# Short-band attention: one transpose for both key blocks, and projections in a planned line of quarters

## The chip, the cores and the metric

The kernel runs on one core of one Trainium2 chip. The metric is the device time of one execution in microseconds; the kernel before took 903.53 us (median of three runs, 901.57 to 904.65).

## What is computed

One block of a transformer over 1024 tokens of width 1024, in float32: a modulated RMS norm, one input projection, two kinds of attention, their gated outputs, and an output projection. Attention A (8 heads in 2 groups) has three branches: compressed, selected, and a window of 512. Attention B, the short band, is the part that the change touches (8 heads in 2 groups of 4, window 128, one learned sink a head):

```
dist  = qpos - kpos
valid = (dist >= 0) & (dist < 128) & (kpos >= 0)
s = q k^T / 8 - slope * dist            where valid, else -1e30
p = softmax([s, sink])[..., :-1]
o = p v
```

A block of 128 queries meets two blocks of 128 keys, the one ahead of it and its own. Query p of the block sees the keys j > p of the block ahead and the keys j <= p of its own: of every two keys at the same column j exactly one is in the window.

## The kernel before

**Numbers.** The products are float32 made of two parts: each operand is split into a high part (rounded to float32r, "hh", "wh", "kh", "ph") and the rest ("hl", "wl", "kl", "pl"). A projection of one half (512 tokens) of one weight block is 24 matmuls of 512 columns: eight slices of the input width times three products (L187, L194, L195). A weight block comes by DMA in two halves of 256 KB (wraw), ACT makes the high part (L161) and POOL the rest (L164). There are three buffers for wraw and six each for wh and wl.

**Units.** Attention runs in four units: B group 0, B group 1, A group 0, A group 1. A unit goes through query blocks i = 0 to 7; a step is one block and branch. `scores` does, for each of the four heads: two matmuls q times kh and kl (L770, L773; 256 columns for B), a DVE reduction that adds the distance table, writes the negated row to SBUF and takes its minimum (L780), and an exponential with row sum on ACT (L792). For B the sink is then brought in by two DVE sums of four columns and an exponential of four columns (L798 to L801), and POOL scales the four rows by the reciprocal (L804). `weigh` then takes each key block: four transposes by TensorE into one bank (L841), the high part by ACT (L847), the rest by DVE (L848), and two matmuls of 512 columns with V into the bank pv (L849, L852). A B step with i > 0 has two key blocks, so eight transposes and four such matmuls. `finish` adds the two halves of pv (L861, L862), multiplies by a gate on POOL (L863) and stores. Of PSUM's banks three are for scores, two for transposes, one for pv and two for projections. Row tiles: tag ps, 4 buffers of 1024 columns, and pw, 4 of 640; the B steps took ps and pw in turn.

**Order.** The order on each engine is fixed before the run by a scheduler with priorities. Scores of step i go ahead of the transposes and products of step i-1, at high priority. Into this go projections that later steps and units need, and gate projections (merge) that are only stored. A planner keeps a clock of attention work (`done`, columns / 2400) and notes in `mark` the matmul at each point. `held(t)` gives the matmul behind which a projection has to stay; `owed` makes a later matmul of the attention stay behind a projection. In the A units a line of projections is cut into quarters (six matmuls each) that are spread over the unit: quarter() keeps each of them behind the attention matmul 3 us of that clock ahead of its place and in front of the one 4 later:

```
            hold[0] = held(at - AHEAD)
...
            owed.append((at + LAG, ins))
```

In the B units whole projections of a half were put behind certain steps instead (`at_step`, `k_fills`, `q_fills`), eight in either unit, three of them merges, with the first bound and without the second.

Of the kernel before, what the change touches and what calls it, by code (L numbers as in the profile page):

```python
# [7 lines left out]
F32 = mybir.dt.float32  # L8
F32R = mybir.dt.float32r
# [5 lines left out]
P = 128  # L15
# [6 lines left out]
LATE = (0.1, 0.1)  # L22
LAG = 4
# [3 lines left out]
AHEAD = 3  # L27
# [41 lines left out]
def hybrid_kernel(tc, io, out):  # L69
# [601 lines left out]
    def load_tables(mixer):  # L671

        tab = at.tile([P, HS + P], F32, name="tab", tag="tab", bufs=1)
        if mixer == "B":
            nc.scalar.dma_start(tab[:, :256], io["DB"])
            tables["DB"] = tab[:, :256]
        else:
            nc.scalar.dma_start(tab[:, : HS + 120], io["DA"])
            tables["DW"], tables["DCMP"] = tab[:, :HS], tab[:, HS : HS + 120]
# [31 lines left out]
    def scores(mixer, g, i, br):  # L711
# [9 lines left out]
        else:  # L721
# [22 lines left out]
            "slc": ("ps", S), "win": ("pw", 640), "cmp": ("pc", 0), "swa": (("ps", S), ("pw", 640))[i % 2]}[br]  # L744
        for r in range(4):
            h = 4 * g + r
            pump()
            if len(rows) < 4:
                q = Q[(mixer, h, half)][:, qo : qo + P]
                row = at.tile([P, width], F32, name=tag, tag=tag, bufs=4)  # L750
                off = 0
                for c, (kh_half, b0, nb) in enumerate(parts):
# [12 lines left out]
                    elif br == "win":  # L765
                        dist = tables["DW"][:, :w]
                    else:
                        d0 = (b0 - (i - 1)) * P
                        dist = tables["DB"][:, d0 : d0 + w]
# [8 lines left out]
                    else:  # L778
                        init = BIGF
                    ins = nc.vector.tensor_tensor_reduce(  # L780
# [4 lines left out]
                    if pre:  # L785
# [41 lines left out]

    def weigh(mixer, g, i, br, tiles, pv, first, last):

        rows, b0 = tiles  # L830
        if br == "cmp":
            weigh_pairs(g, rows, pv)
            return
# [43 lines left out]
    class Planned:  # L877
# [13 lines left out]
        def quarter(self, k, at, nxt):  # L891
# [5 lines left out]
            hold[0] = held(at - AHEAD)  # L897
# [8 lines left out]
            owed.append((at + LAG, ins))  # L906
# [11 lines left out]
    def plan_k(g, half):  # L918
# [6 lines left out]
    n_late = len(late)  # L925
    late_done = [0]
# [6 lines left out]
    for mixer, g in units:  # L933
        columns = 0
        for i in range(NT):
            for br in ["swa"] if mixer == "B" else ["slc", "win", "cmp"]:
                nb = {"swa": min(i, 1), "slc": i, "win": min(i, 4), "cmp": 0}[br] + 1
                columns += 1650 if br == "cmp" else 2048 * nb + 8 * (nb * P + 64 * (br == "slc"))
        whole.append(columns / 2400)

    for u, (mixer, g) in enumerate(units):
# [5 lines left out]
        nt = len(tasks)  # L947
        at_step = {}

        def spread(fs, lo, hi):  # L950
            for n, f in enumerate(fs):
                at_step.setdefault(int(lo + (hi - lo) * n / len(fs)), []).append(f)

        if mixer == "B":
            own = [] if u == 1 else k_fills(mixer, g, 1)
            spread(own + q_fills(mixer, g, 1), 0, 3 * nt // 8)
            m2, g2 = units[u + 1]
            nk = k_fills(m2, g2, 0) if m2 == "A" else []
            spread(nk + q_fills(m2, g2, 0), nt // 2, nt)
        else:  # L960
# [7 lines left out]
            for n, f in enumerate(line):  # L968
                nxt = next((x for x in line[n + 1 :] if x.w is not f.w), None)
                for k in range(4):  # L970
                    pieces.append((begun + whole[u] * (n + k / 4) / len(line),
                                   lambda at, f=f, k=k, nxt=nxt: f.quarter(k, at, nxt)))
# [11 lines left out]
        for n, (i, br) in enumerate(tasks):  # L984
# [22 lines left out]
        with tc.high_priority(offset=PRIO):  # L1007
            second(prev)
        for at, f in pieces:
            f(at)  # L1010
# [245 lines left out]
```

## Time and profile before

| | |
|---|---|
| median of three runs | 903.53 us |
| profiled execution: its own time | 904.5 us |
| its span | 902.7 us |
| PE busy | 893.1 us (99%) |
| DVE, ACT, POOL busy | 539.0, 504.0, 354.8 us |
| mean granted TensorE clock | 0.999 |

The span goes from the first to the last instruction in the trace; the rest of the execution's own time lies around it. Matmuls are pipelined: a row gives 0.39 us for one matmul of 512 columns where the next starts 0.23 us later, so the cost of one is read from the distance of starts. PEld is the loading of weights into TensorE, beside the matmuls.

### The profile page before, as it was taken

Reading aid. Unit: us, or ns where it says so; the run is one execution under the profiler, and the core shown is the slowest. Engines: PE = TensorE matmul, PEld = TensorE weight load, DVE = VectorE, ACT = ScalarE, POOL = GpSimd, SP = SyncE. Lnnn points to the kernel's source line nnn. Section 1 sums busy time; section 2 is a strip of 40 time slices with the busy share of each in tenths; the row PEclk is TensorE's granted clock in tenths of the full one; section 3 lists DMA queues with packets and bytes.
Section 4 is the critical chain, followed back from the end, with each engine's and each line's share of the span. In section 5 each row is a group of like instructions: output and inputs, shape, how many; then the busy total and the mean of one; then the engine's idle time right before and its main releaser. Section 6 shows DMA issues by size and latency. Waiting matters only on the chain.

```text
span 902.7 us, 14354 instructions
## 1 busy us (share of the span) xinstructions
PE 893.1 (99%) x4568; PEld 755.4 (84%) x4568; DVE 539.0 (60%) x1514; ACT 504.0 (56%) x1151; POOL 354.8 (39%) x422
## 2 busy tenths in 40 slices
PE   9999999999999999999999999999999999999997
PEld 7888888888888888888888888888887888887885
DVE  5866763455678577675575577566464362677322
ACT  5467632466587677665666687565564565431111
POOL 0000522364576776443445566443442376100000
PEclk9999999999999999999999999999999999999999
DMA  8873342242234322112212131211202577334432
GB/s 317 297 266 100 129 164 97 86 147 95 82 105 132 102 80 68 51 47 71 71 59 71 68 93 58 70 49 47 82 36 71 208 254 233 112 126 167 134 108 78
DMA packets 66942, 104.51 MB, mean 116 GB/s; under 512 B 7985, under 2 KB 25777, under 8 KB 66866
## 3 DMA queue, kind: packets, MB, share of 16 engines
q1 hardware_dynamic: 65712, 102.36, 34.0%
q10 hardware_dynamic: 1154, 1.23, 0.5%
q8 instruction: 36, 0.59, 0.3%
q14 instruction: 40, 0.33, 0.1%
HBM read 79.97 MB, written 19.92 MB: 111 GB/s over the span
## 4 chain that ended last, share of the span: by engine, by line
PE 99%; DVE 0%; ACT 0%; issue 0%; DVEq 0%; POOLq 0%; ACTq 0%
PE b_pt L841 8%; PE b_pj L900 7%; PE b_pj L904 7%; PE b_pj L905 7%; PE b_pj L187 6%; PE b_pj L195 6%; PE b_pj L194 6%; PE b_s L773 5%; PE b_s L770 4%; PE b_pv L852 4%; PE b_pv L849 4%; PE b_s L1139 1%; PE b_s L1141 1%; PE b_s L1140 1%; PE b_pt L294 1%; PE b_s L1063 1%
## 5 line engine op out<-in xcount | busy, mean ns | idle before, releaser
L164 POOL TENSOR_TENSOR wl<-wraw,wh 128x512 fp32r<-128x512 f32 x102 | 135.2, 1326 | 141.0 <-ACT wh L161 87.9
L848 DVE TENSOR_TENSOR pl<-b_pt,ph 128x512 fp32r<-128x512 f32 x162 | 110.3, 687 | 65.3 <-ACT ph L847 64.5
L847 ACT CAST ph<-b_pt 128x512 fp32r<-128x512 f32 x162 | 93.6, 583 | 64.0 <-PE b_pt L841 51.1
L900 PE MATMUL b_pj<-hh,wh 128*128 128x512 f32 x288 | 117.6, 412 | 0.0
L905 PE MATMUL b_pj<-hh,wl 128*128 128x512 f32 x288 | 114.0, 396 | 0.0
L904 PE MATMUL b_pj<-hl,wh 128*128 128x512 f32 x288 | 113.1, 394 | 0.0
L187 PE MATMUL b_pj<-hh,wh 128*128 128x512 f32 x240 | 94.6, 394 | 1.7 <-DVE gates L244 1.7
L194 PE MATMUL b_pj<-hl,wh 128*128 128x512 f32 x240 | 94.6, 394 | 0.0
L195 PE MATMUL b_pj<-hh,wl 128*128 128x512 f32 x240 | 94.4, 393 | 0.0
L804 POOL TENSOR_SCALAR ps<-ps,rr,gates 128x128 f32<-128x128 f32 (+7 forms) x64 | 52.4, 823 | 94.6 <-DVE rr L796 54.6
L770 PE MATMUL b_s<-kh,q 128*128 128x256 f32 (+6 forms) x272 | 85.4, 322 | 0.2 <-DVE minc L786 0.2
L773 PE MATMUL b_s<-kl,q 128*128 128x256 f32 (+6 forms) x272 | 83.7, 315 | 0.0
L792 ACT ACTIVATE ps<-ps,mins 128x256 f32<-128x256 f32 (+7 forms) x96 | 64.9, 677 | 30.1 <-DVE mins L780 28.4
L161 ACT CAST wh<-wraw 128x512 fp32r<-128x512 f32 x94 | 57.7, 616 | 38.3 <-PE b_pj L194 14.8
L792 ACT ACTIVATE pw<-pw,mins 128x256 f32<-128x256 f32 (+4 forms) x96 | 60.7, 632 | 28.2 <-DVE mins L780 26.6
L852 PE MATMUL b_pv<-pl,V 128*128 128x512 f32 x162 | 67.8, 418 | 0.3
L849 PE MATMUL b_pv<-ph,V 128*128 128x512 f32 x162 | 65.7, 405 | 0.0
L905 PEld LDWEIGHTS b_pj<-hh,wl 128*128 128x128 f32 x288 | 54.1, 188 | 10.8
L904 PEld LDWEIGHTS b_pj<-hl,wh 128*128 128x128 f32 x288 | 54.4, 189 | 8.5
L804 POOL TENSOR_SCALAR pw<-pw,rr,gates 128x640 f32<-128x640 f32 (+4 forms) x64 | 47.3, 742 | 32.9 <-DVE rr L796 25.4
L900 PEld LDWEIGHTS b_pj<-hh,wh 128*128 128x128 f32 x288 | 53.9, 189 | 7.5
L841 PE MATMUL b_pt<-ident,ps 128*128 128x128 f32 x344 | 57.8, 272 | 0.0
(303 smaller groups left out, 2106.9 us busy)
## 6 DMA issues: line engine op xcount, KB each, us to landing
wraw<-in_w_blk SPq DMA_DIRECT2D x90, 256.0 KB, 2.7
wa<-in_w_adaT SPq DMA_DIRECT2D x24, 512.0 KB, 5.2
w1raw<-in_w SPq DMA_DIRECT2D x16, 256.0 KB, 3.6
od<-ot SPq DMA_DIRECT2D x64, 64.0 KB, 2.1
sp_MA<-sp SPq DMA_DIRECT2D x16, 256.0 KB, 2.0
wraw<-in_w_o SPq DMA_DIRECT2D x16, 256.0 KB, 3.0
wraw<-in_w_out SPq DMA_DIRECT2D x16, 256.0 KB, 3.0
t<-od SPq DMA_DIRECT2D x16, 256.0 KB, 3.9
```

The source lines that it names most:

```text
L164: chain("wl", nc.gpsimd.tensor_tensor(wl, raw, wh.bitcast(F32), ALU.subtract))
L187: ins = nc.tensor.matmul(t, lhsT=wh, rhs=hh[kc][half], start=(kc == 0), stop=False)
L194: nc.tensor.matmul(t, lhsT=wh, rhs=hl[kc][half], start=False, stop=False)
L195: nc.tensor.matmul(t, lhsT=wl, rhs=hh[kc][half], start=False, stop=(kc == KC - 1))
L770: ins = nc.tensor.matmul(sp[:, :n_in], lhsT=q, rhs=rh, start=True, stop=False)
L773: nc.tensor.matmul(sp[:, :n_in], lhsT=q, rhs=rl, start=False, stop=True)
L792: nc.scalar.activation(rows[r][:, :off], rows[r][:, :off], AF.Exp, scale=-1.0, bias=last_min[:, r : r + 1], accum_out=sums[:, r : r + 1])
L841: ins = nc.tensor.transpose(t[:, r * P : r * P + P], rows[r][:, off : off + P], ident)
L848: nc.vector.tensor_tensor(pl, t, ph.bitcast(F32), ALU.subtract)
L900: ins = nc.tensor.matmul(self.t, lhsT=wh, rhs=hh[kc][self.half], start=(kc == 0), stop=False)
L904: nc.tensor.matmul(self.t, lhsT=wh, rhs=hl[kc][self.half], start=False, stop=False)
L905: ins = nc.tensor.matmul(self.t, lhsT=wl, rhs=hh[kc][self.half], start=False, stop=(kc == KC - 1))
```

## The change

For a B step with i > 0 the two score blocks are joined before the reduction: DVE copies, by a mask (j > p), the scores of the block ahead over those of the block itself, in PSUM, so that the reduction, exponential, scaling and transposes deal with 128 columns for each head where they had 256. After the transposes ACT and DVE write the high part and the rest side by side into one tile of 1024 columns, and POOL parts it by two `affine_select` into the keys of the block ahead and those of the own block, with zeros elsewhere. Four matmuls of 512 columns follow, as before. The two new tiles are of tag ps; the four rows of a B step now lie in one buffer of pw.

The projections in the B units go by the line of quarters of the A units, with bounds of their own (1.5 us ahead, 2 behind): seven in the first unit, nine in the second, the merges six in all as before. The place of a quarter within its projection moves by a fifth of a quarter in all units. The planner counts a joined weighing as 3100 columns. The distance table of B becomes one block of 128 columns and the mask beside it.

```diff
-LATE = (0.1, 0.1)
-LAG = 4
 WARM = (7, 14, 8, 4)
 KEEP = 2
 WBUFS = 6
-AHEAD = 3
+
+AHEAD = {"B": 1.5, "A": 3}
+LAG = {"B": 2, "A": 4}
 PRIO = 1500
...
             nc.scalar.dma_start(tab[:, :256], io["DB"])
-            tables["DB"] = tab[:, :256]
+            tables["DB"] = tab[:, :P]
+            tables["first"] = tab[:, P : 2 * P].bitcast(mybir.dt.int32)
...
-            "slc": ("ps", S), "win": ("pw", 640), "cmp": ("pc", 0), "swa": (("ps", S), ("pw", 640))[i % 2]}[br]
+            "slc": ("ps", S), "win": ("pw", 640), "cmp": ("pc", 0), "swa": ("pw", 640)}[br]
+        if br == "swa":
+            four = at.tile([P, width], F32, name=tag, tag=tag, bufs=4)
         for r in range(4):
             h = 4 * g + r
             pump()
             if len(rows) < 4:
                 q = Q[(mixer, h, half)][:, qo : qo + P]
-                row = at.tile([P, width], F32, name=tag, tag=tag, bufs=4)
+                row = four[:, r * P : r * P + P] if br == "swa" else at.tile([P, width], F32, name=tag, tag=tag, bufs=4)
...
-                        d0 = (b0 - (i - 1)) * P
-                        dist = tables["DB"][:, d0 : d0 + w]
+                        dist = tables["DB"]
...
+                    if br == "swa" and i:
+
+                        nc.vector.copy_predicated(sp[:, P : 2 * P], tables["first"], sp[:, :P])
+                        pre, w = P, P
...
+    def weigh_joined(g, i, rows, pv):
+
+        pump()
+        t = bank("pt")
+        for r in range(4):
+            ins = nc.tensor.transpose(t[:, r * P : r * P + P], rows[r][:, :P], ident)
+            if r == 0:
+                chain("pt", ins)
+                mark(ins, 3100)
+        own, ahead = (at.tile([P, S], F32R, name="pj", tag="ps", bufs=4) for _ in range(2))
+        nc.scalar.copy(own[:, :512], t)
+        nc.vector.tensor_tensor(own[:, 512:], t, own[:, :512].bitcast(F32), ALU.subtract)
+
+        nc.gpsimd.affine_select(
+            out=ahead, in_=own.bitcast(F32), pattern=[[0, 8], [-1, P]], compare_op=ALU.is_gt, fill=0.0,
+            base=0, channel_multiplier=1)
+        nc.gpsimd.affine_select(
+            out=own, in_=own.bitcast(F32), pattern=[[0, 8], [1, P]], compare_op=ALU.is_ge, fill=0.0,
+            base=0, channel_multiplier=-1)
+        for n, (part, b) in enumerate(((ahead, i - 1), (own, i))):
+            v = V[b][:, 4 + g].rearrange("p a d -> p (a d)")
+            for k in range(2):
+                ins = nc.tensor.matmul(
+                    pv, lhsT=v, rhs=part[:, 512 * k : 512 * k + 512], start=(n == 0 and k == 0),
+                    stop=(n == 1 and k == 1))
+                if n == 0 and k == 0:
+                    chain("pv", ins)
...
+        if br == "swa" and i:
+            weigh_joined(g, i, rows, pv)
+            return
...
-            hold[0] = held(at - AHEAD)
+            hold[0] = held(at - AHEAD[mixer])
...
-            owed.append((at + LAG, ins))
+            owed.append((at + LAG[mixer], ins))
...
-                columns += 1650 if br == "cmp" else 2048 * nb + 8 * (nb * P + 64 * (br == "slc"))
+                weighed = 1650 if br == "cmp" else 3100 if br == "swa" and i else 2048 * nb
+                columns += weighed + (0 if br == "cmp" else 8 * (nb * P + 64 * (br == "slc")))
...
-        if mixer == "B":
-            own = [] if u == 1 else k_fills(mixer, g, 1)
-            spread(own + q_fills(mixer, g, 1), 0, 3 * nt // 8)
-            m2, g2 = units[u + 1]
-            nk = k_fills(m2, g2, 0) if m2 == "A" else []
-            spread(nk + q_fills(m2, g2, 0), nt // 2, nt)
+        if u == 0:
+            line = plan_k(g, 1, "B") + plan_q("B", 0, 1) + merges(2) + plan_q("B", 1, 0)
+        elif u == 1:
+            line = plan_q("B", 1, 1) + merges(2) + plan_k(0, 0) + merges(2) + plan_q("A", 0, 0)
...
+        places = [n / len(line) for n in range(len(line) + 1)]
+        if u == 0:
+            places = [0.1 * n if n < 4 else 0.3 + 0.7 * (n - 3) / (len(line) - 3) for n in range(len(line) + 1)]
+        for n, f in enumerate(line):
+            nxt = next((x for x in line[n + 1 :] if x.w is not f.w), None)
+            for k in range(4):
+                spot = places[n] + (places[n + 1] - places[n]) * (k + 0.2) / 4
+                pieces.append((begun + whole[u] * spot,
+                               lambda due, f=f, k=k, nxt=nxt, mixer=mixer: f.quarter(k, due, nxt, mixer)))
...
-            hold[0] = held(done[0] - AHEAD)
-            for f in at_step.get(n, []):
-                f()
-            now = done[0] - begun
-            while mixer == "B":
-
-                part = ((late_done[0] + 0.5) / n_late - sum(LATE[:u])) / LATE[u]
-                if part > 1 or part * whole[u] > now:
-                    break
-                hold[0] = held(begun + part * whole[u] - AHEAD)
-                late.pop(0).whole()
-                late_done[0] += 1
...
-    j = np.arange(256)[None, :]
-    d = 128 + p - j
-    DB = dist(d, (d < 0) | (d >= 128))
+
+    j = np.arange(P)[None, :]
+    DB = np.concatenate([np.where(j > p, p - j + P, p - j), j > p], axis=1).astype(np.float32)
```

## Rows read from the trace of the kernel before

**Rows 1.** The page's first two parts: busy us of PE, and the granted clock.
```profile
PE 893.1 (99%) x4568; PEld 755.4 (84%) x4568; DVE 539.0 (60%) x1514; ACT 504.0 (56%) x1151; POOL 354.8 (39%) x422
...
PEclk9999999999999999999999999999999999999999
```

**Rows 2.** All waits of PE in the span: us in total, times, longest us.
```profile
PE b_pj L187 <- DVE gates L244: 1.7, 1, 1.7
PE b_pt L294 <- DVE eps L309: 1.0, 1, 1.0
PE b_s L770 <- DVE minc L786: 0.2, 1, 0.2
```

**Rows 3.** Busy us and instructions of each engine in the short-band units, then PEclk, DMA.
```profile
162.00:298.00 136.00, 136.00 (x717) 115.00 (x716) 83.04 (x252) 89.12 (x243) 81.52 (x107) 1.00 0.34 106
```

**Rows 4.** The chain of waits, 160 to 310 us: start us, us, what.
```profile
232.28 0.87 PE b_pt L841 x8
```

**Rows 5.** Timeline of PE, start and us: projections, then scores.
```profile
205.09 0.39 PE L187 MATMUL b_pj<-hh,wh 128*128 128x512 f32 x1
...
207.81 0.39 PE L187 MATMUL b_pj<-hh,wh 128*128 128x512 f32 x1
...
213.54 0.28 PE L770 MATMUL b_s<-kh,q 128*128 128x256 f32 x1
...
214.13 0.28 PE L773 MATMUL b_s<-kl,q 128*128 128x256 f32 x1
```

**Rows 6.** POOL's groups by shape, whole span: count | busy us, mean ns | idle before.
```profile
L164 POOL TENSOR_TENSOR wl<-wraw,wh 128x512 fp32r<-128x512 f32 x102 | 135.2, 1326 | 141.0 <-ACT wh L161 87.9 <-DVE wh L158 33.7 <-PE b_pt L615 7.3
L863 POOL TENSOR_TENSOR ot<-ot,zt 64x512 f32<-64x512 f32 x32 | 41.2, 1287 | 41.7 <-DVE ot L862 41.4 <-DMA wraw<-in_w_blk 0.2
...
L804 POOL TENSOR_SCALAR pw<-pw,rr 128x256 f32<-128x256 f32 x32 | 14.7, 479 | 15.8 <-DVE rr L801 10.9 <-PE b_pv L852 3.5 <-PE b_s L773 1.4
...
L804 POOL TENSOR_SCALAR ps<-ps,rr,gates 128x1024 f32<-128x1024 f32 x8 | 9.6, 1202 | 21.6 <-DVE rr L796 21.6
...
L804 POOL TENSOR_SCALAR ps<-ps,rr 128x128 f32<-128x128 f32 x8 | 2.8, 371 | 3.5 <-DVE rr L801 2.6 <-ACT wh L161 0.9
masks.py:199 POOL TENSOR_SCALAR_AFFINE_SELECT ident<-ident 128x128 f32<-128x128 f32 x1 | 0.3, 292 | 0.1
...
L1248 POOL MEMSET const-bfloat16-1.0<- 128x1 bf16 x1 | 0.1, 101 | 0.0
```

**Rows 7.** DVE's groups by shape, 100 to 310 us, same columns.
```profile
L780 DVE CUSTOM_DVE_ANT_0 pw<-b_s,tab,nsink 128x256 f32<-128x256 f32 x32 | 14.7, 477 | 8.7 <-PE b_s L773 8.5
...
L798 DVE TENSOR_TENSOR rr<-mins,nsink 128x4 f32<-128x4 f32 x16 | 8.4, 527 | 0.5
...
L780 DVE CUSTOM_DVE_ANT_0 ps<-b_s,DC,nsink 128x128 f32<-128x128 f32 x8 | 2.6, 345 | 3.4 <-PE b_s L773 3.3
...
L652 DVE CAST vc<-vcf 128x128 fp32r<-128x128 f32 x2 | 0.4, 224 | 0.0
```

**Rows 8.** Timelines of POOL and DVE: start us, us, engine, line, what.
```profile
228.21 1.84 POOL L804 TENSOR_SCALAR ps<-ps,rr 128x256 f32<-128x256 f32 x4 [1.48 <-DVE rr L801]
...
273.70 1.29 POOL L863 TENSOR_TENSOR ot<-ot,zt 64x512 f32<-64x512 f32 x1 [0.98 <-DVE ot L862]
274.06 2.21 DVE L798 TENSOR_TENSOR rr<-mins,nsink 128x4 f32<-128x4 f32 x1
274.96 1.28 POOL L164 TENSOR_TENSOR wl<-wraw,wh 128x512 fp32r<-128x512 f32 x1
```

**Rows 9.** Tile ph, 214 to 224 us: ns min/median/max, first and last start.
```profile
L847 ACT CAST ph<-b_pt x2: 587/590/592, 217.4 to 217.8; 128x512 fp32r<-128x512 f32 x2
L848 DVE TENSOR_TENSOR pl<-b_pt,ph x2: 684/688/691, 218.0 to 219.1; 128x512 fp32r<-128x512 f32 x2
...
L849 PE MATMUL b_pv<-ph,V x2: 389/389/389, 221.6 to 223.0; 128*128 128x512 f32 x2
```

More of the change, by code (lines that the diff above doesn't have):

```diff
@@ L784, in scores @@
                         chain(tag, ins)
-                    if pre:
+                    if br == "slc" and pre:
                         nc.vector.tensor_tensor_reduce(
@@ L889, in whole, with quarter @@
             self.out(self.name, self.half, proj_half(self.w, self.half, lambda: bank("pj")))
-        def quarter(self, k, at, nxt):
+        def quarter(self, k, at, nxt, mixer):
             if k == 0:
@@ L916, in plan_q, with plan_k @@
                 for p in range(2)]
-    def plan_k(g, half):
+    def plan_k(g, half, mixer="A"):
+        if mixer == "B":
+            return [Planned("KB", half, lambda name, half, t: k_block([("swa", 0), ("swa", 1)], half, None, t), [])]
         return [Planned(f"KA{g}", half, lambda name, half, t: k_block([("slc", g), ("win", g)], half, None, t), [])]
@@ L924, in hybrid_kernel @@
     late = [f for name in SPILL for f in both(name, spill_out)]
-    n_late = len(late)
-    late_done = [0]
     def merges(n):
@@ L946, in hybrid_kernel @@
         tasks = [(i, br) for i in range(NT) for br in brs]
[L947 to L952, printed above, removed]
-        if mixer == "B":
-            own = [] if u == 1 else k_fills(mixer, g, 1)
-            spread(own + q_fills(mixer, g, 1), 0, 3 * nt // 8)
-            m2, g2 = units[u + 1]
-            nk = k_fills(m2, g2, 0) if m2 == "A" else []
-            spread(nk + q_fills(m2, g2, 0), nt // 2, nt)
+        if u == 0:
+            line = plan_k(g, 1, "B") + plan_q("B", 0, 1) + merges(2) + plan_q("B", 1, 0)
+        elif u == 1:
+            line = plan_q("B", 1, 1) + merges(2) + plan_k(0, 0) + merges(2) + plan_q("A", 0, 0)
         else:
@@ L967, in hybrid_kernel @@
                 line += merges(len(late))
[L968 to L972, printed above, removed]
+        places = [n / len(line) for n in range(len(line) + 1)]
[7 more added lines that the diff above has]
+                               lambda due, f=f, k=k, nxt=nxt, mixer=mixer: f.quarter(k, due, nxt, mixer)))
         prev = None
@@ L982, in second @@
                 finish(mixer, g, i, pvs.pop(i))
-        for n, (i, br) in enumerate(tasks):
+        for i, br in tasks:
             with tc.high_priority(offset=PRIO):
@@ L994, in hybrid_kernel @@
             prev = (i, br, tiles)
-            hold[0] = held(done[0] - AHEAD)
-            for f in at_step.get(n, []):
-                f()
-            now = done[0] - begun
-            while mixer == "B":
-                part = ((late_done[0] + 0.5) / n_late - sum(LATE[:u])) / LATE[u]
-                if part > 1 or part * whole[u] > now:
-                    break
-                hold[0] = held(begun + part * whole[u] - AHEAD)
-                late.pop(0).whole()
-                late_done[0] += 1
         with tc.high_priority(offset=PRIO):
             second(prev)
-        for at, f in pieces:
-            f(at)
+        for due, f in pieces:
+            f(due)
         pieces.clear()
```

## The prediction

> **What bounds the kernel now.** I read the page first, from busy shares to clock. PE is busy 893.1 of 902.7 us, and its clock row stands at 9 in all forty slices, so nothing is to be won from the clock [rows 1]. Then the waits of PE: in the whole span PE waits for another engine three times, 2.9 us together, and of these only 0.2 us lies near the stage that changes [rows 2]. Then the busy times of that stage, the two short-band units at 162 to 298 us: PE 136.0 of 136 us, DVE 83.0, ACT 89.1, POOL 81.5 [rows 3]. So in this stage time is a count of what PE is given, as long as nobody lets PE wait. The question is what leaves PE, and whether the work that arrives on POOL and DVE makes a wait where there was none.
>
> **What leaves PE.** A joined step transposes four tiles of 128x128 where a step of two key blocks transposed eight. The chain of waits has eight of them in 0.87 us, 0.109 us each [rows 4]. Seven query blocks in each of two units are joined: 14 x 4 x 0.109 = 6.1 us. All else on PE stays: scores still run over 256 columns, the products with V are four of 512 columns instead of two pairs, and 16 half projections lie in the two units by either line (8 and 8 before, 7 and 9 after). Nothing is hidden here, since PE is the path.
>
> **What POOL gets.** It loses half of 56 scalings: 128x256 takes 0.479 us and 128x128 0.371 [rows 6], 56 x 0.108 = 6.0 us. It gains 28 selections over 128x1024, a size the trace does not have; let one take A. Bounds: the single selection of 128x128 took 0.292 us [rows 6]. With the slope of the scalings (0.371 to 0.479 for 128 elements more, 0.84 ns an element) A = 0.292 + 896 x 0.00084 = 1.05 us. An instruction of one column takes 0.101 us [rows 6]; if the rest of the 0.292 is all slope, 1.50 ns an element, A = 0.101 + 1024 x 0.0015 = 1.64. If each of the eight rows of the pattern starts anew, A = 8 x 0.292 = 2.34. I take 1.05, nearest to the scaling of 128x1024 at 1.202 [rows 6], which reads two more operands. POOL in the stage: 81.5 - 6.0 + 28 x 1.05 = 104.9 us of some 130, 81%. That fits on average.
>
> By stretches it is tighter. One projection is 24 matmuls, and twelve start 2.72 us apart, 0.227 each: 5.45 us. Six score matmuls start 0.118 apart [rows 5]. In the later 0.7 of the first unit (5.6 steps) the new line has four half projections: a step of PE is 8 x 0.118 + 4 x 0.109 + 4 x 0.227 + 4 x 5.45 / 5.6 = 6.18 us. A step of POOL there is four scalings 1.48, the output product 1.29, six low weight halves in 5.6 steps at 1.33 [rows 6], 1.42, and 2A: 4.19 + 2A = 6.29 us. POOL is 0.11 us short in each of 5.6 steps, 0.6 us. In the second unit (nine projections, fourteen halves) PE's step is 8.42 us and POOL's 5.10 + 2A = 7.2: room.
>
> [...]
>
> **What DVE and ACT get.** DVE loses 14 low halves of the transposed tile (0.69 us each) [rows 9] and 56 band reductions shrink from 0.48 to 0.345 [rows 7]. It gains 56 predicated copies PSUM to PSUM of 128x128, which the trace does not have: between 0.224 (a cast of that size in SBUF) and 0.477 (the reduction of twice the columns, from PSUM) [rows 7]; I take 0.3, by the 0.345 of the reduction of equal size. Sum: -9.7 - 7.4 + 16.8, nearly nothing; with the ends -5 to +10 us on an engine that is 83 of 136 us busy. ACT loses 14 copies of 0.59 us [rows 9] and the wider half of 56 exponentials; it needs no price.
>
> **The longer way to the product.** Transpose, ACT copy, DVE rest stay; then come two selections in a row, 2A = 2.1 us, before the second pair of products. What covers it: in the step at 218 us the high half is ready at about 218, and its product starts only at 221.6 [rows 9]; PE worked on projection quarters in between. 2.1 us is less than this 3.6. If the cover were gone, up to 14 x 2.1 = 29 us would show; I put nothing. What is queued behind a waiting product on PE is everything, the next quarters too, since the order is fixed.
>
> The new line also makes a later matmul of the attention follow each quarter (LAG now holds in the short band). It could turn a late weight half into a wait. No row shows PE waiting for weights now [rows 2], and SP's loads stay as many; nothing to 2 us, I take nothing. KB's copies by SP come a fraction of a unit later and are wanted at its middle: nothing.
>
> **The unit edges.** The selected tiles take two of the four ps buffers, which the first rows of the next unit want as well. Before, the odd last step used pw, and the edge cost 0.2 us [rows 2]. Now two heads of the first selected row wait for the product of step 7: nothing to 2A + 0.59 + 0.69 = 3.4 us; I take 1.1, a third, since the step's own transposes are early by then.
>
> **Sum.** -6.1 + 0.6 + 1.1 = -4.4 us. The profiled execution took 904.5, 1.0 above the median of 903.53: 900.1 for it, 899.1 for the median.
>
> **Rivals.**
> *DVE is held by POOL.* The four-column sum after a step's minima takes 0.160 at best and 0.527 in the mean of 16 [rows 7]; at 274.06 it took 2.21 us and ended as two POOL instructions, from 273.70 and 274.96, ended [rows 8]. Both its inputs lie in SBUF. [...] Two such sums stand in each step, and pairs of selections make the longest trains yet. The way from scaling to transposes has about 2.2 us of slack (scaling ends at 228.21 + 1.84, transposes at 232.28) [rows 4, 8]. If both sums of a step wait for a pair, 2.1 us instead of 0.4, the way is 3.4 longer, 0.7 longer by the four copies (4 x (0.3 - 0.13)), 0.4 shorter by the scaling: 1.5 over the slack. In a quarter of 14 steps that is 5.3 us, and -4.4 + 5.3 gives 904.4; from a third of the steps on the kernel is slower. Against it: average waits grow with POOL's share only, from 60 to 81%.
> *The edges cost all of it.* 3.4 instead of 1.1: -2.1 us, 901.4. For it: four ps buffers only. Against: quarters of two units are open there.
> *POOL becomes the bound: slower.* Place: the late part of the first unit, where loss = 5.6 x (2A - 1.99), and from A = 1.66 on the second unit too, 8 x (2A - 3.32). With 1.1 for the edges and 6.1 won it is slower by over 2.7 us from A = 1.67. At 1.64 it stands at 905.7; at 1.9, 10.1 + 3.8 lost, 912.4; at 2.34, 26 lost, 924.5. For it: a pattern of two levels was never run here. Against: the slopes of all POOL rows.
>
> **How the numbers follow.** Forecast 0.55, with a range of its own of 897 to 901 (edges and POOL's shortage at nothing, or both doubled). DVE held 0.13, edges 0.12, POOL the bound 0.15; 0.05 for a better order than now. 0.3% (2.7 us) is about what a measurement of this kernel can tell from no change: faster means below 900.8, slower above 906.2. Faster: nearly all of the forecast, a third of DVE held and of the edges, the 0.05: 0.66. Slower: 0.13 of POOL and a little of DVE held: 0.16. Same: 0.18. The range of 895 to 906 leaves out most of POOL the bound and a few hundredths below.
>
> **What would show it.** Right: transposes of the stage down by 56, no PE wait over 1 us inside it, PE near 100% busy, the stage some 5 us shorter, a selection near 1.05 us. Wrong: selections at 1.6 us or more with PE waiting for their tiles; two-input sums on DVE in the mean above 1 us and PE waiting for scaled rows; a PE gap where the second band unit ends; or PE as busy as before in a stage that is no shorter, which would say that the order of the work and not its amount had changed.

## The result, and the profile after

The changed kernel takes 910.95 us (median of four runs, 909.25 to 912.11) where the kernel before takes 902.75 (four runs on the same chip): ratio 1.0079, 95% interval 1.0059 to 1.0100. It is slower; the prediction said 899.1 and 895 to 906. The times of one kernel fall into two groups some 3 us apart, and the traces place that difference in the first 14 us, ahead of everything that the edits touch, so the medians of a few runs can differ by it.

The page first, as [rows 1]. PE has 56 matmuls fewer, and is busy 98% in place of 99%; the granted clock shows nothing at this grain.

```profile
span 908.5 us, 14244 instructions
...
PE 891.5 (98%) x4512; PEld 751.0 (83%) x4512; DVE 552.5 (61%) x1560; ACT 490.2 (54%) x1133; POOL 379.8 (42%) x450
...
PEclk9999999999999999999999999999999999999999
```

The waits of PE, as [rows 2] (who waited for whom: us in total, times, longest us). There were three; now the longest one lies in the short band and is new.

```profile
PE b_s L772 <- DVE mins L786: 2.8, 1, 2.8
PE b_pj L187 <- DVE gates L244: 1.7, 1, 1.7
PE b_s L772 <- DVE minc L792: 1.5, 2, 1.0
PE b_pt L294 <- DVE eps L309: 1.1, 1, 1.1
PE b_pv L886 <- DVE ot L899: 1.0, 1, 1.0
PE b_pv L889 <- DVE pl L885: 0.9, 4, 0.2
PE b_pt L878 <- POOL pw L810: 0.5, 1, 0.5
...
```

Busy times by stretch, as [rows 3], with the short band first and then the place of that wait (us of PE, PEld, DVE, ACT, POOL, then the granted clock). PE stood for 2.3 of the 3 us from 241, and from 245 to 248 it was busy at a granted clock of 0.50.

```profile
162.00:298.00 136.00, 133.15 (x667) 111.48 (x666) 90.44 (x283) 74.48 (x221) 98.17 (x128) 0.99 0.34 103
238.00:241.00 3.00, 3.00 (x17) 2.53 (x16) 2.62 (x4) 2.23 (x7) 3.00 (x4) 1.00 0.43 142
241.00:244.00 3.00, 0.71 (x5) 0.42 (x3) 2.94 (x5) 0.62 (x2) 1.81 (x2) 1.00 0.34 115
...
245.00:248.00 3.00, 3.00 (x11) 2.52 (x10) 2.95 (x12) 2.17 (x9) 2.53 (x5) 0.50 0.09 25
248.00:249.00 1.00, 1.00 (x6) 0.83 (x5) 0.32 (x2) 0.82 (x3) 0.70 (x3) 0.99 0.32 102
```

The timeline around it, as [rows 8] (start us, us, engine, line, what; in brackets idle time before). The sum of four columns on DVE begins at 239.26 and ends at 242.84, just after the last of these POOL instructions, which follow each other without a pause from 229.91 on. The minima, on which the next score matmul waits (it needs the bank that their reduction reads), stand behind the sum on DVE.

```profile
229.91 1.42 POOL L810 TENSOR_SCALAR pw<-pw,rr 128x128 f32<-128x128 f32 x4 [0.76 <-DVE rr L807]
...
238.18 1.09 POOL L847 TENSOR_SCALAR_AFFINE_SELECT pj<-pj 128x1024 fp32r<-128x1024 f32 x1
...
239.24 1.28 POOL L164 TENSOR_TENSOR wl<-wraw,wh 128x512 fp32r<-128x512 f32 x1
...
239.26 3.58 DVE L804 TENSOR_TENSOR rr<-mins,nsink 128x4 f32<-128x4 f32 x1
...
240.49 1.28 POOL L900 TENSOR_TENSOR ot<-ot,zt 64x512 f32<-64x512 f32 x1
...
241.42 0.28 PE L775 MATMUL b_s<-kl,q 128*128 128x256 f32 x1
...
241.73 1.08 POOL L850 TENSOR_SCALAR_AFFINE_SELECT pj<-pj 128x1024 fp32r<-128x1024 f32 x1
...
244.56 0.51 PE L772 MATMUL b_s<-kh,q 128*128 128x256 f32 x1 [2.85 <-DVE mins L786]
```

The groups of 160 to 320 us by shape, as [rows 6, 7] (count | busy us, mean ns | idle before). Two are surprises: `finish`'s ACT copy (L898) waited 13.9 us for the store of the step before (2.0 in the kernel before, same stretch), and a cast of 128x64 (L507) took 2.6 us (0.181).

```profile
L784 DVE COPY_PREDICATED b_s<-tab,b_s 128x128 f32<-128x128 int32 x56 | 15.5, 290 | 14.4 <-PE b_s L775 14.1
L847 POOL TENSOR_SCALAR_AFFINE_SELECT pj<-pj 128x1024 fp32r<-128x1024 f32 x14 | 15.3, 1091 | 7.5 <-DVE pj L845 6.8 <-DVE rr L804 0.6
...
L804 DVE TENSOR_TENSOR rr<-mins,nsink 128x4 f32<-128x4 f32 x16 | 12.9, 804 | 0.3
...
L898 ACT COPY ot<-b_pv 64x512 f32<-64x512 f32 x15 | 8.7, 582 | 15.2 <-DMA od<-ot 13.9 <-PE b_pv L856 0.6 <-PE b_s L775 0.5
...
L806 DVE TENSOR_TENSOR sums<-sums,rr 128x4 f32<-128x4 f32 x16 | 7.8, 489 | 3.6 <-ACT rr L805 3.5
...
L507 DVE CAST kl<-kc 128x64 fp32r<-128x64 f32 x1 | 2.6, 2598 | 0.0
```

Two of these groups in the kernel before, same stretch:

```profile
L861 ACT COPY ot<-b_pv 64x512 f32<-64x512 f32 x16 | 9.3, 581 | 2.8 <-DMA od<-ot 2.0 <-PE b_pt L841 0.4
...
L800 DVE TENSOR_TENSOR sums<-sums,rr 128x4 f32<-128x4 f32 x16 | 4.0, 253 | 4.0 <-ACT rr L799 3.9
```

The chain of waits, as [rows 4], where the second band unit ends and unit A begins. From the product at 307.55 to the next one at 314.39 every piece belongs to `finish`: product, two issues of the gate load and one of the store on SP, the store, copy, sum. So with one output tile this round took 6.84 us (the closest two products of the band units start 5.74 us apart, at 258.63 and 264.37), and behind the second product stand the scalings of A's first rows, for which PE waits.

```profile
307.55 1.27 POOL ot L900
308.84 0.60 SPq L895
...
309.49 0.60 SPq L895
...
310.14 0.60 SPq L903
...
310.79 2.07 DMA od<-ot
...
312.95 0.59 ACT ot L898
...
313.57 0.69 DVE ot L899
...
314.39 1.29 POOL ot L900
315.68 0.44 POOL ps L810
316.12 0.39 POOL pc L810
316.50 0.44 POOL pw L810
...
316.99 0.33 PE b_pt L878
```

**Where the time went.** I took the distance from each PE matmul's start to the next and compared it with the median distance for its shape. The medians add up to 873.19 us before and 867.09 after: PE was given 6.10 us less, the predicted 6.1. What goes beyond the medians rose from 17.65 to 29.53. The difference, 11.9 - 6.1 = 5.8, is that of the two profiled executions (910.3 and 904.5). The medians of the runs differ by 8.2, because 904.5 lies near the top of the runs before and 910.3 near the bottom of those after.

The table has the same by stretch, for the experiments below too, each from its one profile. Its last column takes in the start, where the profiles differ though nothing changes there: the matmul that starts at 141.69 us in the kernel before starts at 138.9 to 140.0 us in e1, e5, e7, e11 and e12, and at 141.3 to 142.3 in all others. So the stretches are better compared than the whole spans.

| us beyond the medians | 232-252 | 252-300 | 300-350 | 540-720 | whole span |
|---|---|---|---|---|---|
| before | 0.5 | 0.5 | 1.6 | 3.2 | 17.65 |
| after | 5.0 | 0.4 | 6.1 | 5.6 | 29.53 |
| line alone (e2) | 0.5 | 0.3 | 3.1 | 5.6 | 21.83 |
| join alone (e3) | 0.5 | 2.2 | 6.3 | 3.1 | 24.01 |
| sums on ACT (e1) | 1.3 | 1.9 | 5.2 | 5.6 | 25.25 |
| two outputs and gates (e12) | 0.5 | 0.2 | 3.3 | 5.3 | 19.77 |
| two outputs (e15) | 0.6 | 0.2 | 2.2 | 5.2 | 21.26 |
| two gates (e16) | 0.6 | 0.4 | 4.2 | 5.3 | 24.29 |
| other order (e17) | 5.0 | 0.5 | 5.4 | 5.2 | 28.88 |
| other order (e18) | 3.8 | 7.0 | 4.4 | 5.6 | 33.56 |
| join, both repairs (e11) | 0.4 | 2.0 | 1.2 | 3.1 | 15.81 |

So there are three losses: the stand of PE at 241 us (4.5), the passage from the second band unit to unit A (300 to 350 us, 4.5), and unit A itself (540 to 720 us, 2.4).

### The profile page after: what moved, and what is told of

It is laid out like the page before. It is cut to its first block, busy times and chain, and to the rows that moved or that the text cites. A ratio compares the mean times of both kernels' runs of the same rounds, so it can differ in the third digit from the quotient of the medians.

```text
span 908.5 us, 14244 instructions
## 1 busy us (share of the span) xinstructions
PE 891.5 (98%) x4512; PEld 751.0 (83%) x4512; DVE 552.5 (61%) x1560; ACT 490.2 (54%) x1133; POOL 379.8 (42%) x450
## 4 chain that ended last, share of the span: by engine, by line
PE 88%; DVE 5%; POOL 2%; ACT 2%; issue 2%; DMA 1%; SPq 1%; DVEq 0%; POOLq 0%; ACTq 0%
PE b_pj L937 8%; PE b_pj L941 8%; PE b_pj L942 8%; PE b_pt L878 6%; PE b_s L775 4%; PE b_s L772 4%; PE b_pv L889 3%; PE b_pj L187 3%; PE b_pj L195 3%; PE b_pv L886 3%; PE b_pj L194 3%; PE b_s L1163 1%; PE b_s L1161 1%; PE b_s L1162 1%; PE b_pt L294 1%
## 5 line engine op out<-in xcount | busy, mean ns | idle before, releaser
L937 PE MATMUL b_pj<-hh,wh 128*128 128x512 f32 x408 | 165.7, 408 | 0.0
L941 PE MATMUL b_pj<-hl,wh 128*128 128x512 f32 x408 | 161.4, 397 | 0.0
L942 PE MATMUL b_pj<-hh,wl 128*128 128x512 f32 x408 | 161.0, 396 | 0.0
L798 ACT ACTIVATE pw<-pw,mins 128x128 f32<-128x128 f32 (+4 forms) x128 | 70.0, 548 | 52.5 <-DVE mins L786 51.5
L941 PEld LDWEIGHTS b_pj<-hl,wh 128*128 128x128 f32 x408 | 77.3, 189 | 12.5
L937 PEld LDWEIGHTS b_pj<-hh,wh 128*128 128x128 f32 x408 | 77.0, 190 | 11.9
L772 PEld LDWEIGHTS b_s<-kh,q 128*128 128x128 f32 x272 | 51.4, 189 | 12.3 <-issue 4.4
L798 ACT ACTIVATE ps<-ps,mins 128x128 f32<-128x128 f32 (+7 forms) x64 | 49.6, 776 | 18.0 <-DVE mins L786 15.8
L775 PEld LDWEIGHTS b_s<-kl,q 128*128 128x128 f32 x272 | 51.4, 190 | 7.1
L900 POOL TENSOR_TENSOR ot<-ot,zt 64x512 f32<-64x512 f32 x32 | 41.1, 1286 | 30.1 <-DVE ot L899 21.8
```

What stands on the lines that cost most here:

```text
L772: ins = nc.tensor.matmul(sp[:, :n_in], lhsT=q, rhs=rh, start=True, stop=False)
L775: nc.tensor.matmul(sp[:, :n_in], lhsT=q, rhs=rl, start=False, stop=True)
L798: nc.scalar.activation(rows[r][:, :off], rows[r][:, :off], AF.Exp, scale=-1.0, bias=last_min[:, r : r + 1], accum_out=sums[:, r : r + 1])
L937: ins = nc.tensor.matmul(self.t, lhsT=wh, rhs=hh[kc][self.half], start=(kc == 0), stop=False)
L941: nc.tensor.matmul(self.t, lhsT=wh, rhs=hl[kc][self.half], start=False, stop=False)
L942: ins = nc.tensor.matmul(self.t, lhsT=wl, rhs=hh[kc][self.half], start=False, stop=(kc == KC - 1))
```

## The experiments

Ratios are to the kernel before on the same chip, with 95% intervals.

**e1: the two sums of a step on ACT** (eight ACT instructions of one column for the two DVE sums and the exponential of four columns between them), so that DVE has neither sum in these steps.

```diff
-            nc.vector.tensor_tensor(rr, last_min, nsink[:, 4 * g : 4 * g + 4], ALU.subtract)
-            nc.scalar.activation(rr, rr, AF.Exp)
-            nc.vector.tensor_tensor(sums, sums, rr, ALU.add)
+            for r in range(4):
+                k = 40 + 4 * g + r
+                nc.scalar.activation(rr[:, r : r + 1], last_min[:, r : r + 1], AF.Exp, bias=smalls[:, k : k + 1])
+            for r in range(4):
+                nc.scalar.activation(sums[:, r : r + 1], sums[:, r : r + 1], AF.Identity, bias=rr[:, r : r + 1])
```

> The changed kernel with the two sums of four columns on DVE (both inputs in SBUF) made by ACT instead, four columns one at a time. Theory H (a two-input sum on DVE is held while POOL works off a train; at 239 us it took 3.6 us, the scores' banks were not freed, PE stood 2.9 us and its clock fell for 3.4 us): no wait of PE over 1 us before the end of the second band unit, some 4.5 us less than 910.95, about 906.5. Rival P (POOL itself is too slow, its train makes PE wait for selected tiles or weights whatever DVE does): as slow as the changed kernel, 910 to 912, with PE waiting elsewhere in the same stretch. Both leave the 4.5 us at the start of the A units.

907.45 us, ratio 1.0038 [1.0021, 1.0054]. The stand at 241 us is gone, and the clock is full there (1.00 in every window from 238 to 249 us); row of the windows of this kernel:

```profile
241.00:244.00 3.00, 2.81 (x14) 2.25 (x14) 1.94 (x12) 3.00 (x17) 2.17 (x5) 1.00 0.35 93
```

The passage to A keeps its loss (5.2), so the held sum is one cause and not the only one.

**e2: the planned line alone**, each B step with its two blocks as before. **e3: the join alone**, with the projections at their old places (the quarters of the A units too).

```diff
 e2, against the changed kernel
...
-        if br == "swa" and i:
-            weigh_joined(g, i, rows, pv)
-            return
...
 e3, against the changed kernel
...
-            line = plan_k(g, 1, "B") + plan_q("B", 0, 1) + merges(2) + plan_q("B", 1, 0)
...
+            for f in at_step.get(n, []):
+                f()
```

> Half of the change: the planned line of quarters in the band units, but two key blocks weighed one after the other as before (no join, no selection by POOL). Theory E (the line puts the query projections of the first A group last, so that their conversion is late and PE stands some 4.5 us at the start of the A units): 902.75 + 3 to 5 = 906 to 908, waits of PE between 300 and 345 us, none inside the band. Rival J (the loss at the edge comes from the joined tiles, which hold ps buffers, and from POOL): no loss, 902 to 904. Rival L (the line, with its second bound, is the whole loss): 902.75 + 11.9 = 914.

> The other half: joined key blocks and selections by POOL, but whole projections behind certain steps as before. If the join alone is worth its transposes and DVE is not held at a bad place: 902.75 - 6.1 = 896.7. Theory H (DVE held by trains of POOL): one or more waits of PE inside the band, 2 to 6 us together, 899 to 903. Rival J (the joined tiles and POOL cost at the edge too): 904 or more, with waits of PE at 300 to 345 us.

The line alone: 906.35, ratio 1.0039 [1.0022, 1.0055]; PE is busy all of 162 to 298 us, and the loss lies in the passage (1.5 us over the kernel before) and in unit A (2.4). The join alone: 903.58, ratio 0.9988 [0.9969, 1.0006]. It has no stand at 241 us, but PE stands between 298 and 304 us, in part because its products wait for the selections, and the clock falls after it, to 0.50 from 304 to 309 us. A cast L507 is held for 3.9 us here as well, but at 269.7 us, far ahead of that stand. Two windows of e3:

```profile
302.00:304.00 2.00, 1.29 (x4) 0.77 (x4) 0.58 (x6) 1.81 (x10) 2.00 (x4) 0.63 0.52 167
304.00:308.00 4.00, 4.00 (x14) 3.22 (x13) 1.21 (x12) 2.18 (x8) 4.00 (x9) 0.50 0.24 69
```

So each half of the change has a loss of its own: the line costs 3.5 us by itself, and the join, even without the line, loses some 5 of the 6.1 us that it saves.

**e4: A's keys and queries ahead of all merges in the line.**

```diff
-            line = plan_q("B", 1, 1) + merges(2) + plan_k(0, 0) + merges(2) + plan_q("A", 0, 0)
+            line = plan_q("B", 1, 1) + plan_k(0, 0) + plan_q("A", 0, 0) + merges(4)
```

> The changed kernel with the line of the second band unit in another order: key block and the two query blocks of the first A group ahead of the four merge halves, which need only be stored. Theory E: waits of PE between 300 and 345 us fall from 4.5 to under 1.5 us, about 907.5; the wait at 241 us, which lies before the reordered part, stays. Rival J (ps buffers, pv's bank and POOL make the edge): the waits of PE there stay above 3 us, 910 to 912.

912.42, ratio 1.0101 [1.0080, 1.0123]. The expectation was missed. The passage got better (3.0 in place of 6.1), but a second stand came at 268 us, with the clock at 0.57 from 272 to 276: PE's wait for the minima is 5.0 us in three times.

**e5, e6, e7, e9: repairs put together.** e5 has the sums of e1, the casts of kc on ACT, and A's keys and queries ahead of two merges; e6 adds two output and two gate tiles (halves of the partitions in turn); e7 is e5 with A's quarters at their places before the change; e9 is e6 with those places.

```diff
...
-                nc.vector.tensor_copy(klp[:, pre - 64 : pre], kc2[:, 1, keys[r][1], :].bitcast(F32))
+                nc.scalar.copy(klp[:, pre - 64 : pre], kc2[:, 1, keys[r][1], :].bitcast(F32))
...
 e6, e9
...
-        ot = at.tile([64, 512], F32, name="ot", tag="ot", bufs=1)
+        ot = otp[64 * (i % 2) : 64 * (i % 2) + 64]
...
 e7, e9
-                spot = places[n] + (places[n + 1] - places[n]) * (k + 0.2) / 4
+                spot = places[n] + (places[n + 1] - places[n]) * (k + (0.2 if mixer == "B" else 0)) / 4
```

> The changed kernel with everything that was seen held by POOL taken off DVE (the two four-column sums by ACT, and the two copies of the compressed keys into the key tiles by ACT), and the line of the second band unit in the order query of B, two merges, key and query of A, two merges. If theories H and E hold and add up: no PE wait over 1 us from DVE's held instructions, edge under 1.5 us; 907.45 (sums on ACT alone) - 1.3 (copy held at 333 us) - 2 (edge) = 904. Rival C (every fixed wait gives way to another, because POOL is 80% busy and the way of a step is as long as the step): 907 again, with waits at new places such as pv's bank.

> As the last one, and with two output tiles and two gate tiles that steps take in turn (halves of the partitions), so that the evacuation of pv does not wait for the store of the step before. Theory O (with the faster band, the round of evacuate, gate on POOL, store, evacuate is what ends last; it held pv's bank 1.5 us at 268 us and 1.2 at 343 us): another 1 to 3 us less, 901 to 903, no wait of PE for the pv evacuation. Rival: stores are covered, no change, 904.

> As e5, with the places of the quarters in the A units as in the kernel before (the shift by a fifth of a quarter only in the band units). Theory S (the shift puts the same waits of PE at 545 to 567 us and 685 to 703 us into every kernel with the new line, 2.2 us more than before): those waits go, 904 - 2 = 902. Rival: they come from the A units' planner clock starting elsewhere, and stay: 904.

> All repairs together: sums and key copies by ACT, A's query blocks ahead of the last merges, two output tiles, and the quarters of the A units at the places of the kernel before. If the repairs add up: 902.17 (e6) - 2 (the places, e7 against e5 gave 2.5) = 900, some 4 us under the kernel before, of the 6.1 us that leave PE. Rival C (a new wait for each repaired one): 902 to 903.

e5 905.10, ratio 1.0008 [0.9995, 1.0021]; e6 902.17, 0.9973 [0.9960, 0.9987]; e7 902.62, 0.9980 [0.9965, 0.9994]; e9 899.91, 0.9950 [0.9937, 0.9962]. The output tiles are worth some 3 us on top of the sums and casts, the old places some 2.

**e8: the line alone with A's quarters at the old places** (the edit of e7 in e2).

```diff
 in e2
...
-                spot = places[n] + (places[n + 1] - places[n]) * (k + 0.2) / 4
+                spot = places[n] + (places[n + 1] - places[n]) * (k + (0.2 if mixer == "B" else 0)) / 4
```

> The line alone (no join) with the places of the quarters in the A units as before. Theory S: PE waits from 500 us on fall to those of the kernel before, 906.35 - 2 = 904.3, and what is left against before is the edge at 313 to 328 us, 1.3 us. Rival: as slow as the line alone, 906 to 907.

906.09, ratio 1.0022 [1.0010, 1.0035] against 1.0039 without: a gain that the intervals don't part. In the three pairs (e2 to e8, e5 to e7, e6 to e9) the ratio falls by 0.0017, 0.0028 and 0.0023; only those of e5 and e7 lie apart. So the shift of the quarters costs perhaps 2 us; the rest of the line's loss stays.

**e10: the kernel before with the sums, casts and tiles of e6. e11: the join alone with them.**

```diff
 both
...
-            nc.vector.tensor_tensor(sums, sums, rr, ALU.add)
...
+                nc.scalar.activation(sums[:, r : r + 1], sums[:, r : r + 1], AF.Identity, bias=rr[:, r : r + 1])
...
-        zt = at.tile([64, 4, P], F32, name="zt", tag="zt", bufs=1)
+        zt = ztp[64 * (i % 2) : 64 * (i % 2) + 64]
```

> Control: the kernel before with the same three repairs (sums and key copies by ACT, two output tiles), no join, no line. PE has no wait in its band units, so by theory H the repairs are worth nothing here: 904.35 within 1.5 us. Rival: the repairs are gains of their own, 902 or less, and then e9 owes them its gain and not the join.

> The join with whole projections at steps (no line) and the three repairs of the last one. The join alone took 903.58, with 5 us of waits at 298 to 309 us, where the last products of the second band unit wait for selections and no projection is left to cover them. If that lack of cover is the cause, the repairs change little: 902 to 904. If DVE held by POOL was the cause there too: 899 to 900.

e10 903.75, ratio 0.9995 [0.9984, 1.0007]: the repairs are worth nothing where nothing is joined. e11 896.86, ratio 0.9926 [0.9912, 0.9941], the best of all, and against its expectation: the cover that I thought the line gave isn't needed. 0.9995 to 0.9926 is 6.2 us of 904; but from the same matmul near 140 us to the end, ahead of which nothing changes, the two profiles differ by 4.7 us (760.6 and 755.9). So the join, mended, is worth most or all of its transposes. Between e11 and e6 (the line, with the same repairs) lie 0.0047, 4.2 us for the line; between e11 and e9, where the A units have their old places, 0.0024, 2.2 us.

**e12: the changed kernel with two output and two gate tiles, nothing else.**

```diff
...
-        zt = at.tile([64, 4, P], F32, name="zt", tag="zt", bufs=1)
+        zt = ztp[64 * (i % 2) : 64 * (i % 2) + 64]
...
-        ot = at.tile([64, 512], F32, name="ot", tag="ot", bufs=1)
+        ot = otp[64 * (i % 2) : 64 * (i % 2) + 64]
```

> The changed kernel with two output and two gate tiles alone. Theory H: DVE's sum is still held near 240 us, the wait of 2.9 us there stays, only the pv waits (1.2 us) go: 909 to 910.5. Rival: the round through the store delays POOL's trains, and without it the train that holds DVE is broken: 906 or less.

901.18, ratio 0.9976 [0.9964, 0.9988]. The rival's time came out: with every DVE instruction still there, the first sum is short again (the second, at 472 ns, is not), the cast into kl takes 0.181 us (the two into kh 0.882 in the mean, 0.179 before), and there is no stand (160 to 320 us, as above; the changed kernel had 804 and 2598 ns):

```profile
L902 ACT COPY ot<-b_pv 64x512 f32<-64x512 f32 x17 | 9.9, 582 | 7.8 <-PE b_pv L856 7.4 <-issue 0.2
...
L804 DVE TENSOR_TENSOR rr<-mins,nsink 128x4 f32<-128x4 f32 x16 | 7.1, 443 | 0.2
L507 DVE CAST kl<-kc 128x64 fp32r<-128x64 f32 x1 | 0.2, 181 | 0.0
```

**e13 and e14: one repair each in the join alone.** e13 has the tiles of e12, e14 the sums and casts of e5.

```diff
 e13, in e3
...
+        ot = otp[64 * (i % 2) : 64 * (i % 2) + 64]
 e14, in e3
...
+                nc.scalar.activation(sums[:, r : r + 1], sums[:, r : r + 1], AF.Identity, bias=rr[:, r : r + 1])
```

> The joined step with the projections at their old places, and two output and two gate tiles in turn; the sums and casts stay on DVE. Round theory (the step waits for the store of the step before, which packs POOL's work): this alone gives nearly all that both repairs gave (896.9), so 897 to 898.5, and PE's stand and clock fall at 298 to 309 us are gone. Held-DVE theory (it is the DVE instructions behind POOL's trains that count, whatever packs them): 901.5 to 903.5, the cast of 128x64 is still held for over 2 us at the end of the second unit and PE still stands there.

> The joined step with the projections at their old places, and the two sums and the casts of kc on ACT in place of DVE; one output tile and one gate tile as in the changed kernel. Held-DVE theory: 897 to 899, the stand at 298 to 309 us is gone. Round theory: 901 to 903, since the copy of pv still waits for the store and the product with V for the copy.

e13 899.19, ratio 0.9955 [0.9938, 0.9972]; e14 904.11, ratio 0.9995 [0.9980, 1.0010]. In the passage the held DVE instructions are not the cause: without any, e14 has PE standing from 298 to 302 us and at a clock of 0.50 after it, with POOL busy without a break from 287.3 to 303.5 us. In e13 PE still stands for 1 us at 298 us, but its clock holds (1.00 over 296 to 309 us). The tiles carry most of the gain; sums and casts give nothing without them (e14 against e3), and with them perhaps 2 us more (e11 against e13, where the intervals meet). Windows of e14:

```profile
298.00:300.00 2.00, 1.07 (x4) 0.59 (x4) 1.13 (x5) 0.91 (x3) 2.00 (x3) 1.00 0.55 172
300.00:302.00 2.00, 0.92 (x5) 0.36 (x3) 0.60 (x5) 0.17 (x1) 2.00 (x4) 1.00 0.25 66
...
304.00:306.00 2.00, 2.00 (x6) 1.56 (x5) 0.89 (x8) 1.93 (x8) 1.92 (x3) 0.50 0.00 0
```

**e15 and e16: the changed kernel with two outputs or two gates alone.** The tile that stays single still changes its half of the partitions, since its partner does.

```diff
 e15
...
+        zt = at.tile([P, 4, P], F32, name="zt", tag="zt", bufs=1)[lo : lo + 64]
...
+        ot = otp[lo : lo + 64]
 e16
...
+        zt = ztp[lo : lo + 64]
...
+        ot = at.tile([P, 512], F32, name="ot", tag="ot", bufs=1)[lo : lo + 64]
```

> The changed kernel with two output tiles in turn (partition halves of one tile) and a single gate tile. Store theory (what counted with both was that the ACT copy of pv no longer waits for the store of the step before): 901 to 902.5, ACT idle ahead of the copy for the store near nothing, no stand of PE at 241 us. Gate theory (the load of the gate tile behind the product of the step before): 908 to 911, the stand stays.

> The changed kernel with two gate tiles in turn and a single output tile. Store theory: 908.5 to 911 as the changed kernel, the stand at 241 us and ACT's wait for the store stay. Gate theory: 901 to 903.

e15 901.72, ratio 0.9973 [0.9959, 0.9988]; e16 903.01, ratio 0.9993 [0.9978, 1.0009]. The store theory was right on e15 and fell on e16: ACT's copy there still waits 12.7 us for the store, and yet the stand is gone. Row of e16's copy, 160 to 320 us:

```profile
L901 ACT COPY ot<-b_pv 64x512 f32<-64x512 f32 x16 | 9.3, 583 | 16.9 <-DMA od<-ot 12.7 <-POOL pw L810 1.8 <-POOL pj L847 1.6
```

On all four engines e16 starts its instructions in the same order as the changed kernel up to 256 us, so a new order is not the reason either. What its timeline shows instead is a pause: where POOL's product lies on partitions 64 to 127, as every second one does in e12, e15 and e16, POOL idles 0.07 to 0.10 us before it and behind it if it follows without a wait, while on partitions 0 to 63 the next instruction starts 0.01 to 0.05 before the last ends. In that pause the held sum gets in (timeline of e16; wl ends at 239.45, the sum at 239.47, the product starts at 239.53):

```profile
238.16 1.29 POOL L164 TENSOR_TENSOR wl<-wraw,wh 128x512 fp32r<-128x512 f32 x1
...
238.62 0.85 DVE L804 TENSOR_TENSOR rr<-mins,nsink 128x4 f32<-128x4 f32 x1
...
239.53 1.29 POOL L903 TENSOR_TENSOR ot<-ot,zt 64x512 f32<-64x512 f32 x1
...
240.89 1.09 POOL L850 TENSOR_SCALAR_AFFINE_SELECT pj<-pj 128x1024 fp32r<-128x1024 f32 x1
```

**e17 and e18: another order, nothing repaired**, against the thought that any new order would have been rid of the stand.

```diff
 e17
-                spot = places[n] + (places[n + 1] - places[n]) * (k + 0.2) / 4
+                spot = places[n] + (places[n + 1] - places[n]) * (k + 0.3) / 4
 e18
-AHEAD = {"B": 1.5, "A": 3}
+AHEAD = {"B": 1.7, "A": 3}
```

> The changed kernel with every quarter a tenth of a quarter later in its place (0.3 for 0.2): the same work, no repair, another fixed order. Theory of the round and the held DVE: the cause is built into the joined step with one output tile, so 907 to 912, ACT still waits some 10 us ahead of the copy for the store, and PE stands over 1 us at least once. Rival (the stand at 241 us is an accident of one order, and each repair won because it planned the order anew): 900 to 904, as with the single repairs.

> The changed kernel with the bound of the short band at 1.7 us ahead in place of 1.5: the same work, no repair, another fixed order. Theory of the round and the held DVE: 907 to 912 with a stand of PE of over 1 us. Rival (accident of one order): 900 to 904, no stand.

e17 909.59, ratio 1.0059 [1.0041, 1.0078]; e18 914.84, ratio 1.0118 [1.0094, 1.0142]. Both keep the stand, e18 has three. e17 changes no instruction's order before 272 us and repeats the sum to the digit; e18's order differs from 219 us on, and its sum at 240.32 takes 3.58 again. There PE had a quarter of a projection to work on, and stood for 1.8 and then 1.1 us at full clock; after its stand of 2.8 us at 275 us, behind two casts held for 1.2 and 2.4 us, the clock was 0.51. So what a held sum costs depends on the work that PE has ahead of the wait. Row of e17:

```profile
239.61 3.58 DVE L804 TENSOR_TENSOR rr<-mins,nsink 128x4 f32<-128x4 f32 x1
```

## Why the prediction was wrong

**Right: what leaves PE, and the prices.** 6.10 us for the predicted 6.1. A selection took 1.091 us (1.05 taken, 1.64 and 2.34 as bounds), a predicated copy 0.290 (0.3), a reduction 0.348 (0.345). So POOL did not become the bound by its amount: 98.2 us of 136. The longer way to the product cost nothing that shows: no wait of the changed kernel names the selected tiles (e3 has 0.9 us of them, between 298 and 304 us).

**The step that failed: "what DVE and ACT get", summed to nearly nothing.** It left out the two sums of a step, whose mean went from 0.527 and 0.253 us to 0.804 and 0.489: 16 x (0.277 + 0.236) = 8.2 us more on DVE, and with them a wait of PE. That a sum waits for POOL stood in the first rival, at 0.13, and the instruction was the right one. Its path and its price were wrong. The rival followed the way from the sums over the scaling to the transposes, with a slack of 2.2 us; PE stood ahead of that, at a score matmul, because the minima that free its bank stand behind the sum on DVE. And the rival spread the wait over the steps and asked for a third of them to be slower, but one sum was enough: it was held not for a pair of selections (2.1 us) but over three POOL instructions in a row (3.6 us), and the clock was at 0.50 after PE had stood. From the starts on PE: 241.42 to 244.56 where 0.12 is the rule, 3.0 lost; then some 1.7 at a clock of 0.50 until 248.2. "Average waits grow with POOL's share" was the fault of reasoning. POOL's 98.2 us were not spread but came in trains, one of them without a pause from 229.91 to 242.81, 12.9 us; the longest in the kernel before, 162 to 298 us, ran from 248.67 to 254.26, 5.6 us.

The trace has the order of the two: the POOL instruction of 239.24 began ahead of the sum of 239.26, and the sum ended 0.03 us after a POOL instruction did (242.84 and 242.81). It was not sums alone: a cast of 128x64 took 2.598 us where it took 0.181 in the kernel before. Why they wait for POOL, no run shows.

**The unit edges: 1.1 taken, 3.4 as the bound, 4.5 measured.** Most of it was not the two selected tiles in four buffers, which e15 leaves as they are while it gets 3.9 back, but `finish`, which the prediction never priced: product, gate load, store, copy and sum form a round, 6.84 us at 307.55, because one output tile serves all steps. In the prediction's two units a joined step of PE takes 6.18 and 8.42 us, so by that round a late product is made up slowly or not at all. Before, the copy waited 2.0 us for the store in the whole stretch, now 13.9. The join without the line loses as much there (6.3 in e3), the line without the join 3.1 (e2). With two output tiles the passage loses 2.2 in place of 6.1 (e15), with sums moved 5.2 (e1). In the join alone the same holds (e13, e14).

**The line: "nothing to 2 us, I take nothing".** 0.0039 of 904.5 is 3.5 us alone (e2), and some 4.2 with both repairs (e6 against e11). It is 8.2 where nothing is mended (the changed kernel against e3) and 1.9 with the tiles alone (e12 against e13, where the intervals meet): what the line costs depends on what it meets. Perhaps 2 us of it are the fifth of a quarter by which the places in unit A move, which I quoted and did not price. In the changed kernel 2.4 us lie in unit A at 540 to 720 us, and the line alone loses nothing between 232 and 300 us (e2).

**Open.** In e12, e15 and e16 two things changed together: buffers, and the half of the partitions with its pauses in POOL. For the stand at 241 us the pause is the better account, since e16 lost the stand and kept the wait for the store; I had no run that has the one without the other. For the passage, e15 against e16 (2.2 and 4.2) speaks for the store. The step from e14 to e11 helps further: neither has a DVE instruction that is held by over 0.4 us between 160 and 350 us, so a pause that lets one in can't be what they differ by. Yet with the tiles of e11 the time from the matmul near 140 us to the end falls by 4.9 us (760.8 to 755.9), some 4.7 of it between 252 and 350 us. That leaves the buffers, of the output and of the gates together, or the order that was planned anew. Which part of the line costs the rest was not settled.

## What to carry to other kernels

When a step gets shorter, price the rounds that don't: a single buffer whose store has to land before its next writer makes a round, here one of 6.84 us, that no share of busy time shows. When work is moved to GpSimd (POOL), look for trains and not for shares: what counted here was how long it ran without a pause (12.9 us) while a four-column sum of DVE (3.58 us, 0.804 in the mean) stood in front of the minima that PE waited for. And try the parts of a change one by one: here the join was worth some 5 to 6 us once mended, and the line cost 2 to 8 us in every pairing.

## What the runs showed of the hardware

Over all twenty traces, 150 to 345 us, I counted the ends of POOL instructions during which a four-column sum of DVE waited, and took it to have got in where it ended within 0.08 us of that end. Where POOL paused behind the instruction, the sum got in at 124 of 131 ends, and at the other seven it had itself begun less than 0.04 us ahead. Where the next POOL instruction followed at once, it got in at 68 of 106, and some were passed over after 2.5 us of waiting. An ACT instruction of one column took 0.287 us (mean of 64 in e1), so that eight of them take 2.3 us of ACT where DVE's two sums take 0.8 at their means before.
